# A hybrid decoder step on one core: scaling products moved to GpSimd, gate rows asked for a tile earlier, a raw buffer for the output weights, and half of the sample rows' output products ahead

## The chip, the cores and the metric

The kernel runs on one core of a Trainium2 chip. The metric is the device time of one execution in microseconds (us). The core has five engines that work side by side, each through its own queue in order: TensorE (PE, with its weight loads as PEld), VectorE (DVE), ScalarE (ACT), GpSimd (POOL) and SyncE (SP, which here issues most DMAs). SBUF is the working memory of 128 partitions, PSUM the memory into which PE writes.

## The reference, cut to what matters

One inference step for a prompt of 1024 rows and for 8 sample rows with a cache of 1024 rows each. A row goes through one input projection, then through three groups of heads, and through one output projection.

```python
q_raw, kv_raw, g_raw, z_nsa, u_rw, z_rw, q_mem, z_mem = split_in(rms_norm(hp, ln_g[l]) @ w_in[l])
o_nsa = ...    # 8 heads: compressed blocks, selected blocks, a window of 512, mixed by gates
o_rw, sh_p, st_p = rwkv7_mix(u_rw, ...)                     # 4 heads, a recurrence
o_mem = mem_attend(q_mem, mkv_p, mem_q_norm[l])             # 4 heads against 256 memory rows

def mixer_out(o_nsa, z_nsa, o_rw, z_rw, o_mem, z_mem, w_out):
    cat = jnp.concatenate([o_nsa.reshape(b, t, NSA_W) * jax.nn.silu(z_nsa),
                           o_rw * jax.nn.silu(z_rw),
                           o_mem.reshape(b, t, MEM_W) * jax.nn.silu(z_mem)], axis=-1)
    return cat @ w_out
hp = hp + mixer_out(...)
```

The softmaxes are `p = exp(s - m)` and `p / sum(p)`. The division by the sum is the scaling that this change moves between engines.

## The kernel before

There are three phases. Phase 1 (0 to about 515 us) projects all rows and runs the recurrence. Phase 2 (about 515 to 822) is the attention of the prompt rows: eight tiles of 128 rows, from tile 7 down to tile 0, each with four units (a key head and a pair of query heads). For a unit PE makes scores `p_s`, DVE masks them and takes their maximum (L1321), ACT takes the exponential into `p` (L1322), DVE takes the reciprocal of the sum `fac` (L1344), GpSimd scales `p` by it and the gate (L1347), PE transposes it into `p_pT`, DVE or ACT copies that to `pt` (L1294, L1292), PE multiplies by the values into `p_o`, and DVE multiplies the result into `cat` (L1380), which starts out as the gate rows z. Beside the units run smaller pieces as Python generators, which hand over when PE's modelled clock has moved on by the number that they yield: `q_stack` (queries split into a high and a low part, `qhl`, and transposed into `qs`), `attn_cmp` (the compressed branch: scores `p_sc`, softmax `pcq`), `attn_rwkv` (the recurrence's rows `y_rw`, transposed into `p_yT` and multiplied into `cat`, L1280), `attn_mem` (memory attention: `p_sm`, softmax `pmem`, transposed into `p_pTm`), and the sample rows' own small tasks. `load_z` asks for one tile's `y_rw` and gate rows by two DMAs.

Phase 3 (822 to the end) weaves two generators together. `out_prompt` is the output projection of the prompt rows: first the output columns of half 1 with the weights W1, then half 0 with W0. `wo_half` loads and splits the weights of a half in eight pieces k: a DMA into one of three buffers `wor`, a high part `woh` on ACT (L2191) and a low part `wol` on DVE (L2192). `out_rows` makes 24 matmuls `p_out` of a tile and half and adds the residual `xres`. `sample_nsa` is the attention of the sample rows over their cache pages `pg`, in two fours (a = 0, 1); `pages` issues the DMAs of a sample, `squeeze` compresses a sample's cache (`p_hid`), `nsa_four` does four samples' attention from `p_ss` on. At the end `out_proj_sample` zeroes and fills `c_s`, the sample rows' concatenated outputs `cats` in high and low parts, and makes 32 `p_out` matmuls with W0 and with W1, whose pieces are loaded and split a second time, since W0 took over the space of the first.

PE's instructions are kept in the order in which the generators emit them. On the other engines a scheduler sets the order from the same sequence, and pieces marked with a high priority (`first`) come ahead. The order on every engine thus follows from the yields and from the places of the calls.

Of the kernel before, what the change touches and what calls it, by code (L numbers as in the profile page):

```python
# [114 lines left out]
class Step:  # L115
# [1054 lines left out]
    def prompt_cmp(self):  # L1170
# [43 lines left out]
    def q_stack(self, i):  # L1214
        nc = self.nc
        A, G, PE = nc.scalar, nc.gpsimd, self.te
        first = i == 7
        q = self.kt.tile([128, 12, 64], F32, name="q7") if first else self.we.tile([128, 12, 64], F32, name="q", tag="q", bufs=2)
        nc.sync.dma_start(q[:].rearrange("p h d -> p (h d)"), self.q_d[i * 128:(i + 1) * 128, :])
        qs = self.qs[i] = (self.kt if i % 2 else self.wk).tile([128, 12, 128], F32R, name="qs", tag="qs")  # L1220
        for b in (0, 1, 2):
# [2 lines left out]
            A.activation(hl[:, :, 0], q[:, 4 * b:4 * b + 4], AF.Copy)
            (self.nc.vector if i < 3 else G).tensor_tensor(hl[:, :, 1], q[:, 4 * b:4 * b + 4], hl[:, :, 0].bitcast(F32), op=OP.subtract)
# [4 lines left out]
            yield  # L1230

    def load_z(self, i):
        cat = self.cat[i] = self.slot(i, [128, 8, 128], F32, f"cat{i}")
        y = self.y_rw[i] = self.we.tile([128, 256], F32, name="y_rw", bufs=2)
        self.nc.sync.dma_start(y[:], self.y_d[i * 128:(i + 1) * 128, :])
        self.last_z = self.nc.sync.dma_start(cat[:], self.z_d[:, i * 128:(i + 1) * 128].rearrange("(c p) t -> p c t", p=128))

    def attn_cmp(self, i):
# [30 lines left out]
        V.tensor_tensor(pcq[:], pcq[:], bc(rc[:, :, None], [128, 8, 64]), op=OP.mult)  # L1269
        yield 6.0 if i < 7 else 4.0  # L1270
# [111 lines left out]
    def attn_mem(self, i):  # L1382
# [5 lines left out]
        for c in range(2):  # L1388
# [13 lines left out]
            V.tensor_tensor(pm[:], pm[:], bc(sm[:, :, None], [128, 2, 256]), op=OP.mult)  # L1402
# [73 lines left out]
    def phase2(self):  # L1476
        tc, nc, I, O = self.tc, self.nc, self.I, self.O
        with ExitStack() as ctx:
# [77 lines left out]
            for j, (n, a, b) in enumerate(groups):  # L1556
                i, g, hp = units[n]
                self.unit = n
                if a == 0:
                    left = sum(1 for m, _, _ in groups if m == n)  # L1560
                    if (g, hp) == (0, 0):
# [4 lines left out]
                        if i < 7:  # L1566
                            self.load_z(i)
# [615 lines left out]
    def wo_half(self, pool, n, queue):  # L2183
        nc, I = self.nc, self.I
        out = []
        for k in range(8):
            wl = pool.tile([128, 512], F32R, name=f"wol{k}")
            raw = self.wst.tile([128, 512], F32, name="wor")[:]
            self.last_wor = queue.dma_start(raw, I["w_out"][0, k * 128:(k + 1) * 128, n * 512:(n + 1) * 512])
            wh = pool.tile([128, 512], F32R, name=f"woh{k}")  # L2190
            nc.scalar.activation(wh[:], raw, AF.Copy, scale=0.5)  # L2191
            nc.vector.scalar_tensor_tensor(wl[:], raw, 0.5, wh[:].bitcast(F32), op0=OP.mult, op1=OP.subtract)  # L2192
            out.append((wh, wl))
# [32 lines left out]

    def out_proj_sample(self, Ws):

        nc, I, O = self.nc, self.I, self.O
        c = self.op.tile([128, 8, 40], F32R, name="c_s", tag="chi", bufs=2)  # L2230
        z = self.op.tile([128, 8, 40], F32, name="c_z", tag="clo", bufs=2)
        nc.gpsimd.memset(z[:], 0.0)
        nc.gpsimd.tensor_copy(c[:], z[:])
        nc.scalar.activation(c[:, :, 0:NS], self.cats, AF.Copy)
        nc.vector.tensor_tensor(c[:, :, 32:40], self.cats, c[:, :, 0:NS].bitcast(F32), op=OP.subtract)
        for n, W in enumerate(Ws):
            cs = slice(n * 512, n * 512 + 512)
            o = self.op.tile([128, 512], F32, name="xres", bufs=3)
            nc.sync.dma_start(o[:NS], I["x_sample"][:, 0, cs])
            po = self.pP.tile([128, 512], F32, name="p_out", tag="o")  # L2240
            for k in range(8):
                for j in range(2):
                    self.te.matmul(po[:40], c[:, k, :], W[k][j][:], start=(k == 0 and j == 0), stop=(k == 7 and j == 1))
            nc.vector.tensor_tensor(o[:NS], o[:NS], po[:NS], op=OP.add)
            nc.vector.tensor_tensor(o[:NS], o[:NS], po[32:40], op=OP.add)
            nc.sync.dma_start(O["y_sample"][:, 0, cs], o[:NS])
# [8 lines left out]
    def phase3(self):  # L2255
        tc = self.tc
        with ExitStack() as ctx:
# [4 lines left out]
            self.wst = P("wst", 3)  # L2262
# [108 lines left out]
```

## Time and profile before

| | us |
|---|---|
| median of 3 runs (lowest, highest) | 983.46 (983.21, 985.57) |
| the profiled execution, by its own time | 988.05 |
| span of the profiled execution | 986.3 |
| mean granted TensorE clock | 0.993 |

The span goes from the first to the last instruction. A row of the profile names a line of the kernel, an engine, an operation, and its tiles as out<-in. "xN" counts instructions; behind "<-" stands what released a waiting instruction. The table of windows gives each engine's busy time within a stretch, the granted TensorE clock as a share of full speed, the share of time that the DMA engines were busy, and GB/s. The rows themselves stand in the prediction.

### The profile page before, as it was taken

The page shows a single profiled execution, that of the slowest core. Times are in us where ns is not written, and L with a number is a line of the kernel's source. Part 1 is how long each engine was busy: PE and PEld are TensorE (multiplying, and loading weights), DVE is VectorE, ACT ScalarE, POOL GpSimd, SP SyncE. Part 2 cuts the span into 40 slices and gives each one's busy share as a digit, 9 for nine tenths or more (in the row PEclk, how much of TensorE's full clock was granted, in tenths as well). Part 3 has the DMA queues.
Part 4 walks back from the last instruction along what each step waited for, and adds up shares of the span by engine and source line. Part 5 has one row for each costly group of instructions (what it writes and reads, how often), then busy time and mean ns, then how long its engine had stood idle before and what let it go on. Part 6 is the DMA issues. An engine that isn't in the chain of part 4 may idle for free.

```text
span 986.3 us, 24664 instructions
## 1 busy us (share of the span) xinstructions
PE 934.6 (95%) x9851; PEld 788.9 (80%) x9851; DVE 673.2 (68%) x2056; ACT 442.4 (45%) x989; POOL 153.3 (16%) x222
## 2 busy tenths in 40 slices
PE   7999999999999998999998999989999998999997
PEld 7998888878888887788876878878878885877874
DVE  6769579756683997643448668765879986357465
ACT  6664224233522333223435666646577565224212
POOL 2000000000000000000004332423244542112010
PEclk9999999999999999999999999999999999999999
DMA  8321314212221144147148223321210127984512
GB/s 287 105 68 39 92 32 121 76 46 74 74 90 36 39 139 98 45 132 187 44 120 241 94 74 122 126 77 40 54 36 16 61 76 203 300 280 162 161 66 77
DMA packets 133835, 103.81 MB, mean 105 GB/s; under 512 B 34577, under 2 KB 121112, under 8 KB 133592
## 3 DMA queue, kind: packets, MB, share of 16 engines
q1 hardware_dynamic: 128760, 90.53, 31.5%
q0 software_dynamic: 3200, 10.49, 3.2%
q8 instruction: 78, 1.28, 0.5%
q10 hardware_dynamic: 1760, 1.21, 0.4%
q14 instruction: 37, 0.30, 0.1%
HBM read 83.61 MB, written 22.78 MB: 108 GB/s over the span
## 4 chain that ended last, share of the span: by engine, by line
PE 67%; DVE 15%; ACT 7%; DMA 5%; issue 3%; SPq 2%; POOL 0%; ACTq 0%; DVEq 0%; POOLq 0%
PE p_pr L87 20%; PE p_pr L284 8%; PE p_out L87 5%; PE p_pT L87 5%; PE p_s L87 5%; PE p_o L87 4%; ACT p L1322 3%; PE p_hid L87 2%; DMA x<-in_x_prompt_dram 2%; PE p_iy L87 2%; PE p_z L87 1%; DVE p L1321 1%; PE p_it L87 1%; DVE pt L1294 1%; PE p_sc L87 1%
## 5 line engine op out<-in xcount | busy, mean ns | idle before, releaser
L87 PE MATMUL p_pr<-h,whi 128*128 128x512 f32 (+5 forms) x928 | 231.0, 340 | 0.1
L87 PEld LDWEIGHTS p_pr<-h,whi 128*128 128x128 f32 (+1 forms) x928 | 147.3, 184 | 18.8 <-issue 2.7
L87 PE MATMUL p_pr<-h,wlo 128*128 128x512 f32 (+5 forms) x464 | 152.5, 329 | 0.0
L1347 POOL TENSOR_SCALAR p<-p,fac,gates 128x640 f32<-128x640 f32 (+7 forms) x128 | 109.4, 866 | 162.9 <-DVE fac L1344 104.2
L1322 ACT ACTIVATE p<-p,nm 128x640 f32<-128x640 f32 (+7 forms) x128 | 93.0, 728 | 61.4 <-DVE nm L1321 52.8
L87 PEld LDWEIGHTS p_pr<-h,wlo 128*128 128x128 f32 (+1 forms) x464 | 85.1, 183 | 9.6
L284 PE MATMUL p_pr<-h,whi 128*128 128x256 f32 (+2 forms) x416 | 86.8, 304 | 0.4 <-ACT whi L273 0.3
L87 PE MATMUL p_pT<-ident,p 128*128 128x128 f32 x528 | 72.6, 281 | 8.6 <-DVE cat L1280 2.7
L87 PEld LDWEIGHTS p_pT<-ident,p 128*128 128x128 f32 x528 | 57.4, 141 | 20.6 <-issue 8.7
L1321 DVE CUSTOM_DVE_ANT_0 p<-p_s,bmask 128x512 f32<-128x512 f32 (+7 forms) x96 | 60.3, 663 | 13.5 <-PE p_s L87 6.2
L284 PEld LDWEIGHTS p_pr<-h,whi 128*128 128x128 f32 x416 | 66.1, 188 | 3.6 <-ACT whi L273 0.7
L87 PE MATMUL p_o<-pt,vs 128*64 128x128 f32 x1056 | 67.9, 277 | 0.4 <-DVE shid L1009 0.4
L87 PE MATMUL p_s<-kh,qs 128*128 128x512 f32 (+3 forms) x191 | 66.6, 361 | 1.3 <-DVE nm L1321 1.3
L274 DVE TENSOR_TENSOR wlo<-wraw,whi 128x1024 fp32r<-128x1024 f32 (+1 forms) x34 | 40.7, 1197 | 36.1 <-ACT whi L273 36.1
L87 PEld LDWEIGHTS p_o<-pt,vs 128*64 128x64 f32 x1056 | 57.0, 137 | 7.5 <-issue 4.4
L284 PE MATMUL p_pr<-h,wlo 128*128 128x256 f32 (+2 forms) x208 | 62.6, 303 | 0.0
L998 POOL MEMSET w2d<- 128x128 f32 x1 | 0.2, 206 | 399.2 <-PE p_yy L87 399.2
L87 PE MATMUL p_s<-kl,qs 128*128 128x512 f32 (+3 forms) x192 | 61.3, 339 | 0.0
L273 ACT ACTIVATE whi<-wraw 128x1024 fp32r<-128x1024 f32 (+1 forms) x35 | 36.3, 1038 | 50.1 <-PE p_pr L87 36.7
L1294 DVE COPY pt<-p_pT 128x512 f32<-128x512 f32 (+1 forms) x72 | 47.9, 669 | 10.7 <-PE p_pT L87 9.5
L87 PE MATMUL p_out<-woh,chi 128*128 128x512 f32 x128 | 53.7, 419 | 1.3 <-ACT woh L2191 1.3
L87 PE MATMUL p_out<-wol,chi 128*128 128x512 f32 x128 | 51.9, 406 | 1.2 <-DVE wol L2192 0.9
(534 smaller groups left out, 1936.0 us busy)
## 6 DMA issues: line engine op xcount, KB each, us to landing
wraw<-in_w_in_dram SPq DMA_DIRECT2D x34, 512.0 KB
pg<-in_c_pool_dram SPq DMA_DIRECT2D x40, 256.0 KB
pg<-in_c_pool_dram SPq DMA_DIRECT2D x48, 128.0 KB
x<-in_x_prompt_dram SPq DMA_DIRECT2D x8, 512.0 KB
z_d<-zt SPq DMA_DIRECT2D x16, 256.0 KB
cat<-z_d SPq DMA_DIRECT2D x8, 512.0 KB
wor<-in_w_out_dram SPq DMA_DIRECT2D x16, 256.0 KB
xres<-in_x_prompt_dram POOLq DMA_DIRECT2D x16, 256.0 KB, 3.7
```

Source lines behind the costliest of these rows:

```text
L87: self.last = getattr(self.engine, op)(*a, **k)
L273: nc.scalar.activation(hi[:, :, :n], raw[:, :, :n], AF.Copy)
L274: (low or nc.vector).tensor_tensor(lo[:, :, :n], raw[:, :, :n], hi[:, :, :n].bitcast(F32), op=OP.subtract)
L284: self.last_mm = self.pe.matmul(ps[:m, :b - a], w[:, k, :m], h[k][:, a:b], start=(k == 0 and i == 0), stop=(k == 7 and i == 2))
L998: nc.gpsimd.memset(w2d[:], 0.0)
L1294: nc.vector.tensor_copy(pt[:, :n], ps[:, :n])
L1321: V.tensor_tensor_reduce(halves(x), halves(ps), m, -1.0, 3.0e38, op0=OP.add, op1=OP.min, accum_out=nm[:, h, b:b + 1])
L1322: A.activation(x, x, AF.Exp, scale=-1.0, bias=nm[:, h, b:b + 1], accum_out=sm[:, h, b:b + 1])
L1347: nc.gpsimd.tensor_scalar(x, x, f[:, h, b:b + 1], gate[:, hd + h, 1 + b:2 + b], op0=OP.mult, op1=OP.mult)
```

## The change

1. Scaling moves from DVE to GpSimd: `pmem`'s (one product of 128x512 becomes two of 128x256, by the reciprocal and a constant `one`), `pcq`'s for the tiles 6 to 0, and the subtraction of `qhl` for the tiles 2 to 0 (it was on GpSimd already for the others).
2. `load_z` is called for tile i-1 when tile i begins, with three `y_rw` buffers for two, and `attn_cmp` yields 7 for 6.
3. In phase 3 W1's eight pieces are loaded into one raw buffer `wraw`, each in a place of its own. Later two samples' value pages use it, so that `big` has 5 slots for 7, and samples 4 and 5 load their pages by two DMAs each.
4. `sample_cats` fills the second half of `c_s` (k 4 to 7, the recurrence's and the memory's columns) after the first four samples. W1's pieces 4 to 7 are loaded again and split during the second four, and pieces 0 to 3 later. `out_proj_sample` makes the products of k 4 to 7 for both halves, then fills k 0 to 3 and makes the rest.

```diff
@@ q_stack
-            (self.nc.vector if i < 3 else G).tensor_tensor(hl[:, :, 1], q[:, 4 * b:4 * b + 4], hl[:, :, 0].bitcast(F32), op=OP.subtract)
+            G.tensor_tensor(hl[:, :, 1], q[:, 4 * b:4 * b + 4], hl[:, :, 0].bitcast(F32), op=OP.subtract)
@@ load_z
-        y = self.y_rw[i] = self.we.tile([128, 256], F32, name="y_rw", bufs=2)
+        y = self.y_rw[i] = self.we.tile([128, 256], F32, name="y_rw", bufs=3)
@@ attn_cmp
-        V.tensor_tensor(pcq[:], pcq[:], bc(rc[:, :, None], [128, 8, 64]), op=OP.mult)
-        yield 6.0 if i < 7 else 4.0
+        (G if i < 7 else V).tensor_tensor(pcq[:], pcq[:], bc(rc[:, :, None], [128, 8, 64]), op=OP.mult)
+        yield 7.0 if i < 7 else 4.0
@@ attn_mem
-            V.tensor_tensor(pm[:], pm[:], bc(sm[:, :, None], [128, 2, 256]), op=OP.mult)
+            for h in range(2):
+                G.tensor_scalar(pm[:, h, :], pm[:, h, :], sm[:, h:h + 1], self.one[:], op0=OP.mult, op1=OP.mult)
@@ phase2
-                        if i < 7:
-                            self.load_z(i)
+                        if i == 7:
+                            self.load_z(6)
+                        if i > 0 and i < 7:
+                            self.load_z(i - 1)
@@ sample_nsa
+            raw = ctx.enter_context(tc.tile_pool(name="wraw", bufs=1, reuse_waits="tile", side="right")).tile(
+                [128, 2, 2048], F32, name="wraw")
+            self.W1 = self.wo_half(self.wo_tiles(self.wop), 1, nc.sync, range(8),
+                                   lambda k: raw[:, k // 4, k % 4 * 512:k % 4 * 512 + 512])
...
-                big = xp.tile([128, 7, 2048], F32, name="pg")
+                big = xp.tile([128, 5, 2048], F32, name="pg")
...
-                        load(4)
-                        load(5)
+                        for s in (4, 5):
+                            self.pages(s, big[:, 5 - s], raw[:, s - 4])
+                            X[s], KV[s] = big[:, 5 - s], kvs(raw[:, s - 4])
...
+                        again = [self.k1p.tile([128, 2048], F32R, name="wob", tag=f"k{j}") for j in (0, 2)]
+                        parts = iter([x[:, k * 512:k * 512 + 512] for x in again for k in range(4)])
+                        W1 = self.wo_half(lambda name: next(parts), 1, nc.sync, range(4, 8),
+                                          lambda k: big[:, 0, k * 512:k * 512 + 512])
...
                     if a == 0:
+                        self.sample_cats()
                         yield None
-            W1 = self.wo_half(ctx.enter_context(P("wop2")), 1, nc.sync)
+            W1 |= self.wo_half(self.wo_tiles(ctx.enter_context(P("wop2"))), 1, nc.sync, range(4))
@@ wo_half
+            raw = self.wst.tile([128, 512], F32, name="wor")[:] if raws is None else raws(k - ks[0])
@@ out_proj_sample
+        for a in (4, 0):
+            if a == 0:
+                self.split_sample(0, 4)
+            for n, W in enumerate(Ws):
+                po = pos[n]
+                for k in range(a, a + 4):
+                    for j in range(2):
+                        self.te.matmul(po[:40], self.c_s[:, k, :], W[k][j], start=(k == 4 and j == 0), stop=(k == 3 and j == 1))
```

In the new order the lines of the kernel have moved by a few: what was L1280 is L1282, L1347 is L1349, L1402 is L1405, L2189 is L2204.

**DVE, tile 4 of the prompt attention**, before: the end of the window branch of a sample task (`rs_s`, `w_p`), the end of the compressed branch (`c_s`, `c_r`, `pcq`), then the recurrence's rows into `cat`.

```order
L1699 TENSOR_REDUCE rs_m<-p_wS 128x1
L1259 TENSOR_TENSOR pcq<-p_sc,c_m 128x512
L1344 RECIPROCAL fac<-sm 128x2
L1702 RECIPROCAL rs_s<-rs_s 128x1
L1704 TENSOR_TENSOR rs_s<-rs_s,gr 128x1
L1705 TENSOR_SCALAR w_p<-w_p,rs_s 128x512
L1263 TENSOR_REDUCE c_s<-pcq 128x8
L1266 TENSOR_SCALAR c_r<-c_s 128x8
L1267 RECIPROCAL c_r<-c_r 128x8
L1268 TENSOR_TENSOR c_r<-c_r,gates 128x2x4
L1269 TENSOR_TENSOR pcq<-pcq,c_r 128x512
L1280 TENSOR_TENSOR cat_8885<-cat_8885,p_yT 128x256
```

The same place on DVE in the changed kernel, from the reduction of the window branch on:

```order
L1704 TENSOR_REDUCE rs_m<-p_wS 128x1
L1282 TENSOR_TENSOR cat_8136<-cat_8136,p_yT 128x256
L1707 RECIPROCAL rs_s<-rs_s 128x1
L1709 TENSOR_TENSOR rs_s<-rs_s,gr 128x1
L1710 TENSOR_SCALAR w_p<-w_p,rs_s 128x512
L1323 ISA p,nm<-p_s,bmask 128x640
L1323 ISA nm 128x1
L1259 TENSOR_REDUCE c_m<-p_sc 128x8
```

The product into `cat` now follows the reduction directly, and the compressed branch begins only after it.

**GpSimd, tile 2 of the prompt attention** (its p products are 128x384), in the changed kernel. Before, there stood sixteen p products in a row here and nothing else.

```order
L1349 TENSOR_SCALAR p<-p,fac,gates 128x384 x2
L1405 TENSOR_SCALAR pmem<-pmem,sm_m,one 128x256 x2
L1349 TENSOR_SCALAR p<-p,fac,gates 128x384 x2
L1405 TENSOR_SCALAR pmem<-pmem,sm_m,one 128x256 x2
L1227 TENSOR_TENSOR qhl<-q,qhl 128x4x64
L1349 TENSOR_SCALAR p<-p,fac,gates 128x384 x4
L1227 TENSOR_TENSOR qhl<-q,qhl 128x4x64
```

The products of pmem and the subtractions of qhl now stand between the p products, each of which has to wait for those ahead of it.

**SyncE, the start of phase 3**, in the changed kernel: the last weights of the compression, W1's eight pieces, the sample rows' new values, and the first page of a sample (a load of its number, then the DMA).

```order
L1238 DMA cat_11007<-z_d 128x8x128
L960 DMA w1a<-in_cmp_w_dram 128x8x64 x4
L2204 DMA wraw<-in_w_out_dram 128x512 x8
L1889 DMA v_new<-out_dram 32x2x128 x4
L1852 TENSOR_LOAD pt
L1856 ISA
L1856 DMA pg<-in_c_pool_dram 128x2x256
```

Before, the four v_new DMAs stood ahead of the weights, and the eight weight loads, into `wor`, each had their own wait.

More of the change, by code (lines that the diff above doesn't have):

```diff
@@ L1133, in key_pools @@
         self.bmask = self.kt.tile([128, 1152], BF, name="bmask")
+        self.one = self.kt.tile([128, 1], F32, name="one")
         self.qs, self.pcT, self.y_rw, self.turn, self.cat = {}, {}, {}, 0, {}
@@ L1175, in prompt_cmp @@
         G.memset(self.bmask[:], 0.0)
+        G.memset(self.one[:], 1.0)
         V.tensor_copy(self.bmask[:, 0:128], am[:, 128:256])
@@ L1890, in sample_nsa @@
             with P("snsx") as xp:
-                big = xp.tile([128, 7, 2048], F32, name="pg")
-                at = {1: (0, 2), 2: (1, 3), 3: (0, 4), 4: (1, 5), 5: (0, 6)}
+                big = xp.tile([128, 5, 2048], F32, name="pg")
+                at = {1: (0, 2), 2: (1, 3), 3: (0, 4)}
                 kvs = lambda x: x.rearrange("p (n c) -> p n c", n=8)
@@ L2180, in sample_rwkv, with wo_half, wo_tiles @@
         yield
[L2183 to L2193, printed above, removed]
-        return out
+    def wo_half(self, tiles, n, queue, ks=range(8), raws=None):
+        nc = self.nc
+        out = {}
+        for k in ks:
+            wl, wh = tiles(f"wol{k}"), tiles(f"woh{k}")
+            raw = self.wst.tile([128, 512], F32, name="wor")[:] if raws is None else raws(k - ks[0])
+            self.last_wor = queue.dma_start(raw, self.I["w_out"][0, k * 128:(k + 1) * 128, n * 512:(n + 1) * 512])
+            nc.scalar.activation(wh, raw, AF.Copy, scale=0.5)
+            nc.vector.scalar_tensor_tensor(wl, raw, 0.5, wh.bitcast(F32), op0=OP.mult, op1=OP.subtract)
+            out[k] = wh, wl
+        return out
+    def wo_tiles(self, pool):
+        return lambda name: pool.tile([128, 512], F32R, name=name)[:]
     def out_rows(self, W, hi, lo, rows, x, dst):
@@ L2201, in out_rows @@
             for j, (c, w) in enumerate(((hi, wh), (hi, wl), (lo, wh))):
-                self.te.matmul(po[:rows], c[:, k, :rows], w[:], start=(k == 0 and j == 0), stop=(k == 7 and j == 2))
+                self.te.matmul(po[:rows], c[:, k, :rows], w, start=(k == 0 and j == 0), stop=(k == 7 and j == 2))
             if k < 7:
@@ L2225, in out_proj_prompt, with sample_cats @@
             yield
-    def out_proj_sample(self, Ws):
[L2229 to L2246, printed above, removed]
+    def sample_cats(self):
+        x = self.k1p.tile([128, 2048], F32R, name="c_s", tag="k1")
+        self.c_s = x[:, 0:320].rearrange("p (c s) -> p c s", s=40)
+        self.nc.gpsimd.tensor_scalar(self.c_s, self.cd[:].rearrange("p (c s) -> p c s", s=40), 0.0, 0.0, op0=OP.mult, op1=OP.add)
+        self.split_sample(4, 8)
@@ new lines, in split_sample @@
+    def split_sample(self, a, b):
+        nc, c = self.nc, self.c_s
+        nc.scalar.activation(c[:, a:b, 0:NS], self.cats[:, a:b], AF.Copy)
+        nc.vector.tensor_tensor(c[:, a:b, 32:40], self.cats[:, a:b], c[:, a:b, 0:NS].bitcast(F32), op=OP.subtract)
+    def out_proj_sample(self, Ws):
+        nc, O = self.nc, self.O
+        pos = [self.pP.tile([128, 512], F32, name="p_out", tag="o") for _ in Ws]
+        os = [self.op.tile([128, 512], F32, name="xres", bufs=3) for _ in Ws]
+        for n, o in enumerate(os):
+            nc.sync.dma_start(o[:NS], self.I["x_sample"][:, 0, n * 512:n * 512 + 512])
+        for a in (4, 0):
[6 more added lines that the diff above has]
+                        self.te.matmul(po[:40], self.c_s[:, k, :], W[k][j], start=(k == 4 and j == 0), stop=(k == 3 and j == 1))
+                if a == 0:
+                    o = os[n][:NS]
+                    nc.vector.tensor_tensor(o, o, po[:NS], op=OP.add)
+                    nc.vector.tensor_tensor(o, o, po[32:40], op=OP.add)
+                    nc.sync.dma_start(O["y_sample"][:, 0, n * 512:n * 512 + 512], o)
@@ L2248, in out_prompt @@
     def out_prompt(self):
         yield from self.out_proj_prompt(1, self.W1)
-        self.W0 = self.wo_half(self.wop, 0, self.nc.gpsimd)
+        self.W0 = self.wo_half(self.wo_tiles(self.wop), 0, self.nc.gpsimd)
         self.half = 1
@@ L2261, in phase3 @@
             self.tk = self.wk
-            self.wst = P("wst", 3)
+            self.wst = P("wst", 3, side="right")
             self.wop = P("wop", 1)
@@ L2268, in phase3 @@
             self.pP = P("pP3", 2, space=PSUM)
-            self.W1, self.half = self.wo_half(self.wop, 1, tc.nc.sync), 0
+            self.half = 0
             self.te = InOrder(tc, tc.nc.tensor, None)
```

## The prediction

> **What bounds the kernel now.** I read the busy shares and the chain first, to see which engine a change has to help.
>
> ```profile
> PE 934.6 (95%) x9851; PEld 788.9 (80%) x9851; DVE 673.2 (68%) x2056; ACT 442.4 (45%) x989; POOL 153.3 (16%) x222
> PE 67%; DVE 15%; ACT 7%; DMA 5%; issue 3%; SPq 2%; POOL 0%; ACTq 0%; DVEq 0%; POOLq 0%
> ```
>
> TensorE (PE) is busy 95% of the span, and no edit takes a matmul away. A gain can only come out of the time in which PE waits or runs at a lower clock. GpSimd (POOL) looks free at 16%, but that is an average. So the next view is the windows, for the stages that the change touches: the end of the prompt attention (760 to 820), the start of phase 3 (820 to 860) and its second four samples (920 to 940).
>
> ```profile
> core 0: us, PE busy (x) PEld busy (x) DVE busy (x) ACT busy (x) POOL busy (x), PEclk, DMA share, GB/s
> 760.00:780.00 20.00, 18.63 (x199) 16.66 (x199) 19.84 (x52) 13.39 (x38) 14.02 (x13) 1.00 0.10 35
> 780.00:800.00 20.00, 18.11 (x186) 15.77 (x182) 19.03 (x70) 13.65 (x44) 10.03 (x16) 1.00 0.38 107
> 800.00:820.00 20.00, 18.14 (x203) 15.38 (x203) 16.63 (x80) 11.91 (x46) 7.47 (x16) 1.00 0.37 86
> 820.00:840.00 20.00, 17.28 (x112) 11.73 (x107) 12.59 (x25) 9.99 (x17) 3.99 (x7) 0.93 0.73 215
> 840.00:860.00 20.00, 20.00 (x115) 17.50 (x114) 5.48 (x11) 3.75 (x7) 2.17 (x4) 0.99 0.97 311
> 920.00:940.00 20.00, 19.31 (x111) 14.71 (x111) 6.91 (x16) 4.16 (x8) 2.17 (x4) 1.00 0.55 168
> ```
>
> From 760 to 820 VectorE (DVE) is busy 55.5 of 60 us and POOL already 31.5 of 60, while PE idles 5.1 us. Which waits carry PE's idle time after 500 us says the view of waits:
>
> ```profile
> PE p_pT L87 <- DVE cat L1280: 2.7, 1, 2.7
> PE p_out L87 <- DVE c_s L2235: 2.5, 1, 2.5
> PE p_pT L87 <- DVE pcq L1269: 2.4, 1, 2.4
> PE p_out L87 <- ACT woh L2191: 1.3, 3, 0.8
> PE p_ss L87 <- DMA pg<-in_c_pool_dram: 0.7, 1, 0.7
> ```
>
> The first is in tile 4 of the prompt attention, the second at the very end, the fourth at the start of phase 3; the change reaches all three. The third belongs to tile 7, whose pcq product stays on DVE, and remains. The fifth is one that the change may lengthen.
>
> **First output weights.** W1 comes through three buffers `wor`, so its fourth load waits for the first split.
>
> ```profile
> 816.79 2.45 SPq L1880 DMA_DIRECT2D v_new<-out_dram  x4
> 819.34 13.50 SPq L2189 DMA_DIRECT2D wor<-in_w_out_dram  x8
> 833.42 37.01 SPq L1851 DMA_DIRECT2D pg<-in_c_pool_dram  x32
> ```
>
> ```profile
> 830.03 0.63 ACT L2191 ACTIVATE woh<-wor 128x512 fp32r<-128x512 f32 x1 [1.06 <-DMA wor<-in_w_out_dram]
> 830.69 0.69 DVE L2192 SCALAR_TENSOR_TENSOR wol<-wor,woh 128x512 fp32r<-128x512 f32 x1 [1.04 <-ACT woh L2191]
> ```
>
> ```profile
> 827.10:837.90 10.80, 8.57 (x25) 4.31 (x26) 0.00 (x0) 0.97 0.69 201
> 837.90:840.50 2.60, 2.60 (x8) 2.01 (x7) 0.69 (x1) 0.50 0.96 269
> 840.50:846.00 5.50, 5.50 (x26) 4.55 (x25) 0.69 (x1) 0.99 1.02 345
> ```
>
> The first two fences are SyncE's queue and the two halves of a split, each with what it waited for; the third cuts out the p_out matmuls alone. The eight loads take 13.50 us to issue, ACT waits for each (1.06 us in the row), and 25 matmuls need 10.80 us where 26 need 5.50 a little later. So 10.80 less 25 x 0.21, or 5.5 us, is lost, and then 2.60 us go at a granted clock of 0.50, which loses 1.3 more. Now the eight loads go into `wraw` without waiting for each other and stand ahead of v_new on SyncE's queue, so they issue from about 816.8. 2.1 MB at the 311 GB/s of the row of 840 to 860 are 6.7 us: they land by about 826, or up to 5 us later if GpSimd's three W0 and three xres loads (1.6 MB) share the DMA engines all along. DVE's halves then set the pace: 8 x 0.69 = 5.5 us beside its other work, about as fast as PE uses them. I take back 0.3 for that: **-6.5 us**, between 0 (the loads are late all the same) and -6.8. v_new and the pages move along: the pages start near 823 rather than 833.42, and the 128 KB pages of samples 4 and 5, which now take two issues each, are needed only after 900, so they cost nothing unless SyncE stays busy past that time.
>
> **The gap in tile 4.** DVE, in order, does the end of the compressed branch before it comes to the product that ends PE's longest wait:
>
> ```profile
> 651.66 0.69 DVE L1269 TENSOR_TENSOR pcq<-pcq,c_r 128x512 f32<-128x512 f32 x1
> 652.27 0.41 DVE L1280 TENSOR_TENSOR cat<-cat,p_yT 128x256 f32<-128x256 f32 x1
> 652.74 1.05 PE L87 MATMUL p_pT<-ident,p 128*128 128x128 f32 x4 [2.69 <-DVE cat L1280]
> 650.00:655.00 5.00, 2.31 (x11) 2.26 (x11) 3.94 (x10) 0.60 (x1) 1.08 (x1) 0.79 0.00 0
> 655.00:660.00 5.00, 4.97 (x56) 4.33 (x55) 3.04 (x9) 2.72 (x6) 1.74 (x2) 0.87 0.01 3
> ```
>
> In the changed order cat<-p_yT comes ahead of that chain, since its cat was asked for a tile earlier and pcq's product is on GpSimd. Of the 2.69 us I count **-2.5**. The half clock behind it, 5 x 0.21 + 5 x 0.13, is another **-1.7**. What is late next there is the window branch's w_p (L1705), which in the new order follows cat<-p_yT.
>
> The clock row bears on a rule: the half clock in 650 to 660 comes after an idle time of 2.69 us. The Trainium skill, "TensorE: Matmul & The Clock Gate", "What's actually happening", gives an idle window of about 3.4 us as what lowers the clock; by that page's rule this gap would not lower it, and the clock terms (1.7 and 1.3) would not hang on these gaps. The trace disagrees in this place: the gap is shorter and the clock fell.
>
> **Scaling on GpSimd.** What moves, and what the nearest operations take:
>
> ```profile
> L1402 DVE TENSOR_TENSOR pmem<-pmem,sm_m 128x512 f32<-128x512 f32 x16 | 12.2, 760 | 0.2
> L1269 DVE TENSOR_TENSOR pcq<-pcq,c_r 128x512 f32<-128x512 f32 x8 | 6.1, 767 | 0.1
> L1225 DVE TENSOR_TENSOR qhl<-q,qhl 128x256 fp32r<-128x256 f32 x9 | 3.7, 415 | 5.3 <-ACT qhl L1224 5.3
> L1347 POOL TENSOR_SCALAR p<-p,fac,gates 128x256 f32<-128x256 f32 x16 | 10.4, 667 | 10.7 <-DVE fac L1344 7.8 <-PE p_q L87 2.9
> L1225 POOL TENSOR_TENSOR qhl<-q,qhl 128x256 fp32r<-128x256 f32 x12 | 8.8, 731 | 31.8 <-PE p_s L87 19.2 <-ACT qhl L1224 12.5
> ```
>
> DVE loses 12.2 + 7 x 0.767 + 3.7 = 21.3 us. In tiles 2 to 0, the stretch from 760 to 820, that is 3 x (2 x 0.76 + 0.767 + 3 x 0.415) = 10.6 of its 55.5. PE idles 5.1 us there, the most that this can give back; the least is nothing. I take **-1.5**, since only part of that idle time ends with DVE.
>
> GpSimd gets 32 pmem halves (nearest row: 0.667 us each), 9 subtractions (0.731) and 7 pcq products of 128x512, which it doesn't do before: between one 128x256 product (0.731) and more than two of them (1.46 and up, to 2.4 if blocked); I take 1.2. For tiles 2 to 0 that is 12 x 0.667 + 9 x 0.731 + 3 x 1.2 = 18.2 us on top of 31.5, so 49.7 of 60. It fits, but p's own scaling, for which PE's transposes wait, now queues behind these: waits of **+1.5** in all, between 0 and what the rival below gives.
>
> ```profile
> L1347 POOL TENSOR_SCALAR p<-p,fac,gates x13: 559/686/1707, 760.9 to 779.6; 128x384 f32<-128x384 f32 x12, 128x256 f32<-128x256 f32 x1
> ```
>
> This row of line 1347 alone, for 760 to 780, has the minimum, median and maximum of one operation: 0.56 to 1.71 us, nearly all of one shape. GpSimd is slowed up to 2.5 times where DVE is never idle. The Trainium skill, "SBUF — State Buffer", "Who interferes with whom", says that a DVE instruction with two SBUF inputs and a GpSimd one that reads SBUF exclude each other for the whole instruction, which speaks against this part of the change. The trace agrees in size; by that rule, if every added operation met such an instruction, the sum would be the rival's, below.
>
> At the last tile the order changes too: two pmem halves stand before the last two p products and two after, 2 x 0.667 where DVE took 0.76: **+0.7**, as nothing else covers it. The memset of `one`, and c_s's zeroing after the first four samples, lie on GpSimd where it idles: nothing.
>
> **Second four samples and end.** Four W1 loads are inserted on SyncE among the last value pages, for which p_ss waits already.
>
> ```profile
> 645.10 0.43 SPq L1236 DMA_DIRECT2D cat<-z_d  x1
> 913.44 21.07 SPq L1855 DMA_DIRECT2D pg<-in_c_pool_dram  x24
> ```
>
> A load costs SyncE 0.43 us in the nearest row for a plain one, and 0.88 as a page: 1.7 to 3.5 us, or nothing if the pages are early now. I take **+1.7**. Their splits (4 x 0.63 on ACT, 4 x 0.69 on DVE) lie in 920 to 940, where DVE is busy 6.91 of 20; if that cover were gone they would cost 2.8.
>
> ```profile
> 973.91 0.67 DVE L2207 TENSOR_TENSOR xres<-xres,p_out 128x512 f32<-128x512 f32 x1
> 974.78 0.43 PE L87 MATMUL p_out<-woh,c_s 128*40 128x512 f32 x1 [2.47 <-DVE c_s L2235]
> 980.13 4.00 SPq L2246 DMA_DIRECT2D out_dram<-xres  x2
> ```
>
> PE waits 2.47 us for c_s. Now 16 matmuls of k 4 to 7 (3.5 us at 0.22) stand in that wait; the second half's PSUM buffer comes free only when the xres add ends (974.58), some 0.5 us of waiting. So **-2.0**, between 0 and -2.5.
>
> **Sum:** -6.5 - 2.5 - 1.7 - 1.5 + 1.5 + 0.7 + 1.7 - 2.0 = -10.3 us. The profiled execution took 988.05 (span 986.3), so it would be 977.8; the median of the runs is 4.6 lower than it, and the same -10.3 gives 983.46 - 10.3 = **973.2**.
>
> **Rivals.** 0.3%, 2.95 us, is about what a measurement can tell from no change: faster ends at 980.5, slower begins at 986.4.
>
> 1. *Phase 2 gives its part back.* The new order makes other gaps, with half clocks behind them, for the one it closes. For it: DVE's 55.5 of 60 leave every order tight. Against: pmem and pcq are used late. Then only -6.5 + 1.7 - 2.0 = -6.8 is left, 976.7, to 979 with one gap of 2.5 more. Chance 0.22.
> 2. *W1 is still late:* wraw's space comes free only after the last p_s, and eight loads compete with W0, xres and the pages (DMA share 0.97 in 840 to 860). Half of the 6.5 would go: 976.5, or 979.7 if all of it does. It is also the case in which the change doesn't do what it says. Chance 0.12.
> 3. *GpSimd becomes the bound in tiles 2 to 0*, the slower side. The 18.2 added us fit if they stretch less than (60 - 31.5)/18.2 = 1.57 times; at the 2.5 times of the row (1707 to 686) they are 45.5, 77 of 60, so that phase lasts 17 us longer. With the other terms (-6.5 - 2.5 - 1.7 + 0.7 + 1.7 - 2.0 = -10.3): +6.7, 990. Against it: most p rows have the median, not the maximum; at 2.1 times it is even. Chance 0.14, of which 0.10 slower.
>
> The forecast has 0.52. **Faster** gets 0.52 + 0.20 + 0.06, **same** 0.02 + 0.06 + 0.04, **slower** 0.10. The range goes from 966 (DVE's relief whole, the p_ss wait and the GpSimd waits nothing: -3.6 - 1.7 - 1.5) to 982, which takes in both phase-3-only cases and a mild form of rival 3.
>
> **What would show it.** The p_out group near 820 to 835 has no waits for woh, and pages start near 823; if ACT waits for `wraw`, rival 2. No wait of p_pT for cat<-p_yT and a clock of 1.00 in tile 4; new waits over 2 us between 515 and 820 mean rival 1, and p_pT waiting for POOL's p with POOL over 55 of 60 means rival 3. p_ss waits for a page near 2.4 us. The last p_out matmuls follow p_oT directly. I am wrong as a whole if GpSimd's 128x512 product takes far over 1.2 us, or if PE's half clocks come at new places.

## The result, and the profile after

| | before | changed |
|---|---|---|
| median of 5 runs each on one chip, us | 983.46 | 978.97 |
| lowest to highest | 983.21 to 986.12 | 976.72 to 983.03 |
| ratio changed to before, 95% interval | | 0.9942 (0.9918 to 0.9966) |
| the profiled execution, its own time | 988.05 | 983.03 |
| its span | 986.3 | 981.3 |
| its mean granted TensorE clock | 0.993 | 0.984 |

The kernel is faster by 4.5 us, or 0.58%; the forecast was 10.3 us. The profiled execution of the changed kernel is the longest of its five, with the lowest clock (the others had 0.989 to 0.995). First the busy shares and the chain of the changed kernel:

```profile
PE 939.0 (96%) x9851; PEld 796.3 (81%) x9851; DVE 656.6 (67%) x2025; ACT 443.1 (45%) x990; POOL 178.9 (18%) x270
PE 72%; DVE 15%; ACT 6%; DMA 3%; issue 2%; SPq 1%; POOL 0%; DVEq 0%; ACTq 0%; POOLq 0%
```

GpSimd took 25.6 us more, DVE 16.6 less, and PE's share of the chain rose. PE's longest waits after 500 us:

```profile
PE p_ss L87 <- DMA pg<-in_c_pool_dram: 2.6, 1, 2.6
PE p_PT L87 <- DVE s_sel L1710: 2.5, 2, 1.9
PE p_pT L87 <- DVE pcq L1271: 2.3, 1, 2.3
...
PE p_sm L87 <- DVE pt L1296: 1.3, 1, 1.3
...
PE p_pT L87 <- POOL p L1349: 1.0, 1, 1.0
```

The waits for cat (2.7) and c_s (2.5) are gone, and that for woh has fallen from 1.3 to 0.5. The wait of p_ss has become the longest, 2.6 for 0.7 us, and p_sm waits for a pt copy (near 600 us) where no such wait stood. SyncE's queue and the p_out matmuls at the start of phase 3:

```profile
812.50 6.20 SPq L2204 DMA_DIRECT2D wraw<-in_w_out_dram  x8
818.81 3.44 SPq L1889 DMA_DIRECT2D v_new<-out_dram  x4
822.90 25.99 SPq L1856 DMA_DIRECT2D pg<-in_c_pool_dram  x20
826.10:831.60 5.50, 5.38 (x24) 4.48 (x25) 0.00 (x0) 1.00 1.04 330
```

The eight loads issue in 6.20 us, the pages follow at 822.90, and 24 p_out matmuls take 5.50 us at full clock. The windows of the granted clock, and the end, first the p_oT matmul of the profile before, then the changed kernel:

```profile
520.50:530.70 10.20, 10.20 (x33) 8.40 (x33) 7.78 (x17) 5.46 (x11) 3.81 (x4) 0.50 0.86 241
930.10:933.50 3.40, 0.85 (x7) 0.00 (x1) 0.63 (x2) 0.00 (x0) 0.02 (x1) 1.00 0.52 189
933.50:936.90 3.40, 3.37 (x9) 1.74 (x10) 0.00 (x0) 0.00 (x0) 0.51 (x1) 0.50 0.23 77
936.90:940.30 3.40, 3.40 (x17) 2.81 (x17) 2.75 (x13) 0.42 (x1) 0.00 (x0) 1.00 0.00 0
```

```profile
972.03 0.27 PE L87 MATMUL p_oT<-ident,oS 128*128 128x128 f32 x1
```

```profile
968.98 0.27 PE L87 MATMUL p_oT<-ident,oS 128*128 128x128 f32 x1
969.00 0.47 PE L87 MATMUL p_out<-woh,c_s 128*40 128x512 f32 x1
971.58 2.05 PE L87 MATMUL p_out<-wob,c_s 128*40 128x512 f32 x8 [0.49 <-DVE xres L2224]
976.95 2.15 SPq L2274 DMA_DIRECT2D out_dram<-xres  x2
```

Just behind the wait of p_ss the clock goes to 0.50 for one window of 3.4 us. 10 us at half clock also stand from 520.5 to 530.7, where the profile before had none; PE is busy all through them. At the end the matmuls follow p_oT at once, with the wait of 0.49 for the xres add.

### The profile page after: what moved, and what is told of

Its sections match the earlier page's. It is cut to its first block, busy times and chain, and to the rows that moved or that the text cites. A ratio compares the mean times of both kernels' runs of the same rounds, so it can differ in the third digit from the quotient of the medians.

```text
span 981.3 us, 24739 instructions
## 1 busy us (share of the span) xinstructions
PE 939.0 (96%) x9851; PEld 796.3 (81%) x9851; DVE 656.6 (67%) x2025; ACT 443.1 (45%) x990; POOL 178.9 (18%) x270
## 4 chain that ended last, share of the span: by engine, by line
PE 72%; DVE 15%; ACT 6%; DMA 3%; issue 2%; SPq 1%; POOL 0%; DVEq 0%; ACTq 0%; POOLq 0%
PE p_pr L87 20%; PE p_pr L284 7%; PE p_out L87 6%; PE p_s L87 6%; PE p_pT L87 4%; PE p_o L87 4%; PE p_hid L87 3%; ACT p L1324 2%; DVE p L1323 2%; PE p_iy L87 2%; PE p_sc L87 2%; PE p_z L87 1%; PE p_it L87 1%; PE p_mo L1077 1%; PE p_w L203 1%
## 5 line engine op out<-in xcount | busy, mean ns | idle before, releaser
L1349 POOL TENSOR_SCALAR p<-p,fac,gates 128x640 f32<-128x640 f32 (+7 forms) x128 | 103.7, 821 | 108.5 <-DVE fac L1346 62.1
L273 ACT ACTIVATE whi<-wraw 128x1024 fp32r<-128x1024 f32 (+1 forms) x35 | 36.3, 1038 | 50.4 <-PE p_pr L87 36.7
```

The source lines that it names most:

```text
L273: nc.scalar.activation(hi[:, :, :n], raw[:, :, :n], AF.Copy)
L1349: nc.gpsimd.tensor_scalar(x, x, f[:, h, b:b + 1], gate[:, hd + h, 1 + b:2 + b], op0=OP.mult, op1=OP.mult)
```

## The experiments

Each group of kernels (e1 to e4, e5 to e8, e9 to e12) ran on a chip of its own, and each ratio is to the kernel before in the same group. The last columns come from the mean granted clock c that each run lists: T x (1 - c) is the time that PE lost if it was the bound all along, and twice that by 3.41 us, the length of one window in the traces, the number of windows at half clock. Within one kernel, over all 206 runs, a run with one microsecond more of T x (1 - c) is 0.64 us longer (correlation 0.79). "At full clock" is the mean time less 0.64 x T x (1 - c); errors are standard errors of the mean. The 0.64 is a correlation, and a late transfer could lengthen a run and lower its clock at once; the one direct test is e12 against e11. The count also takes in half clock behind PE's last matmul, where it costs nothing (in e4's profile 1.0 of 7.8 us). The 81 runs before are those of the three groups, with medians of 986.1, 986.3 and 985.5.

| kernel | runs | median us | ratio to before, 95% interval | mean us | half-clock windows | mean at full clock |
|---|---|---|---|---|---|---|
| before | 81 | 986.0 | | 986.2 ± 0.3 | 3.8 ± 0.2 | 982.0 ± 0.2 |
| changed (first 5 runs and e4; ratio of e4) | 17 | 979.0 | 0.9936 (0.9909, 0.9963) | 980.1 ± 0.8 | 5.9 ± 0.6 | 973.7 ± 0.4 |
| e1 phase 2 alone | 12 | 984.1 | 0.9969 (0.9946, 0.9991) | 983.7 ± 0.7 | 4.2 ± 0.5 | 979.1 ± 0.4 |
| e2 phase 3 alone | 12 | 982.2 | 0.9955 (0.9931, 0.9978) | 982.5 ± 0.8 | 5.2 ± 0.5 | 976.8 ± 0.4 |
| e3 W1 behind pages | 12 | 980.0 | 0.9931 (0.9903, 0.9959) | 980.6 ± 1.0 | 5.7 ± 0.8 | 974.5 ± 0.5 |
| e5 scaling alone | 6 | 982.2 | 0.9952 (0.9933, 0.9971) | 982.2 ± 0.6 | 4.3 ± 0.6 | 977.4 ± 0.4 |
| e6 z ahead alone | 12 | 984.5 | 0.9984 (0.9967, 1.0001) | 984.9 ± 0.6 | 4.3 ± 0.6 | 980.2 ± 0.4 |
| e7 filled wait | 6 | 979.7 | 0.9919 (0.9892, 0.9945) | 978.9 ± 1.2 | 3.9 ± 0.7 | 974.6 ± 0.7 |
| e8 W1 by GpSimd's queue | 6 | 979.7 | 0.9935 (0.9910, 0.9959) | 980.1 ± 1.1 | 5.4 ± 0.8 | 974.2 ± 0.6 |
| e9 changed, no z ahead | 6 | 978.7 | 0.9924 (0.9895, 0.9953) | 978.6 ± 0.6 | 4.9 ± 0.4 | 973.2 ± 0.5 |
| e10 W1 behind, GpSimd splits | 12 | 986.7 | 1.0009 (0.9987, 1.0030) | 986.1 ± 0.7 | 6.9 ± 0.3 | 978.6 ± 0.5 |
| e11 e9 with e10 | 12 | 984.7 | 0.9992 (0.9970, 1.0014) | 985.5 ± 0.7 | 7.2 ± 0.5 | 977.7 ± 0.4 |
| e12 e11, tile 7 filled | 12 | 983.5 | 0.9975 (0.9956, 0.9994) | 983.6 ± 0.6 | 5.5 ± 0.3 | 977.5 ± 0.4 |

**The two halves of the change (e1, e2).** e1 has only the edits 1 and 2 of the change, e2 only 3 and 4.

> Only the edits of phase 2 (scaling on GpSimd, z rows a tile ahead); phase 3 as before. Theory 1 (the prediction's sum): -1.8 us from waits and -1.7 where a half clock went, so about 980 to 982 beside 983.46. Theory 2 (the profile of the changed kernel: phase 2 lasted 304.9 us for 307.4 although it held 8.5 us of half clock loss for 3.4): the waits alone save 7 to 8 us, so 976 to 977 in runs with a mean clock as high as before, and more where the clock is lower. Theory 3 (phase 2 gave its part back): 983 or more.

> Only the edits of phase 3; phase 2 as before. Theory 1: -6.5 for W1, +1.7 at p_ss, -2.0 at the end, so about 976.7. Theory 2 (the profile of the changed kernel, counted from p_new to the end): 159.7 for 163.8 us, so -4 us, 979.4, because p_ss waits 2.6 us and not 0.7, with a half clock behind it. The first pages after W1 must start within 5 us of the end of phase 2 under both.

At full clock the halves are worth 3.0 and 5.2 us, and the whole 8.3, with errors of about 0.4 each: they add up. Theory 1 has the size of e2 at full clock (-6.8 without the 1.3 of the half clock is -5.5). Theory 2 for e1 is too large, and so was its reading of one profile: a span of 304.9 with half clocks subtracted isn't a price. Measured as they run, with their half clocks, e1 gives 2.5 and e2 3.7 us on the means.

**The same kernel again (e4).**

> The changed kernel once more, unaltered, with a profile of its own. If half clocks fall at random places from run to run, this profile has them at other places than 520 to 531, 537, 817, 896 and 933 us, and runs with a lower mean clock are longer by about half of a half-clock window (1.7 us) each. If they hang on the gaps that the change made, they are at the same places.

Its profiled execution has a span of 974.8 us at a clock of 0.992. The half clock at p_ss is there again, one window longer, that near 817 and 896 isn't:

```profile
922.00:925.10 3.10, 0.98 (x10) 0.07 (x3) 0.86 (x2) 0.37 (x1) 0.00 (x0) 1.00 0.69 246
925.10:931.90 6.80, 5.90 (x16) 3.78 (x17) 1.87 (x8) 0.42 (x1) 0.54 (x1) 0.50 0.11 41
```

So both expectations hold in part: most half clocks stand behind places where PE does little, and which of these places gets one changes from execution to execution. Not all do. The rows below are e4's, and then those of e7, a kernel described further down:

```profile
512.20:515.60 3.40, 1.75 (x9) 1.10 (x7) 3.40 (x25) 1.29 (x6) 0.00 (x0) 1.00 0.38 121
519.00:522.40 3.40, 2.57 (x15) 1.59 (x14) 3.32 (x7) 1.84 (x4) 0.11 (x1) 0.99 1.01 265
522.40:525.80 3.40, 3.40 (x7) 2.30 (x8) 2.42 (x6) 3.40 (x8) 2.70 (x3) 0.51 1.06 325
```

```profile
689.90:693.30 3.40, 3.40 (x30) 3.11 (x28) 1.76 (x6) 0.26 (x2) 0.89 (x2) 1.00 0.19 52
693.30:696.80 3.50, 3.50 (x27) 3.19 (x28) 2.06 (x7) 1.74 (x5) 0.00 (x0) 0.51 0.96 246
```

In e4 the clock stayed at 1.00 after 3.4 us in which PE was busy 1.75, and fell after 3.4 us in which it was busy 2.57; in e7 it fell where the profile shows no idle time of PE at all. What else lowers it these runs don't show. Runs of the changed kernel go from 976.6 to 986.9 us.

**Scaling and z ahead apart (e5, e6, e9).** e5 takes the GpSimd edits alone, e6 the z edits alone, and e9 undoes the z edits in the changed kernel:

```diff
-        y = self.y_rw[i] = self.we.tile([128, 256], F32, name="y_rw", bufs=3)
+        y = self.y_rw[i] = self.we.tile([128, 256], F32, name="y_rw", bufs=2)
-                        if i == 7:
-                            self.load_z(6)
-                        if i > 0 and i < 7:
-                            self.load_z(i - 1)
+                        if i < 7:
+                            self.load_z(i)
-        yield 7.0 if i < 7 else 4.0
+        yield 6.0 if i < 7 else 4.0
```

> Only the scaling products on GpSimd (pmem, pcq, qhl); z rows, yields and phase 3 as before. Theory 1 (the prediction's terms: -1.5 for DVE, +1.5 for waits behind GpSimd, +0.7 at the last tile): +0.7 us against before. Theory 2: DVE's relief is worth more, -2 us or better, since p_q and p_pTm no longer wait for DVE. The gap of 2.7 us in tile 4 goes already here if it hung on the pcq chain on DVE, and stays if it hung on where cat<-p_yT stands.

> Only the z rows a tile ahead and the yield of 7; scaling and phase 3 as before. Theory 1: the gap in tile 4 goes, -2.5 us, and with it its half clock. Theory 2: the pcq chain still stands ahead on DVE in another tile, and the gap comes back elsewhere: within 1 us of before.

> The changed kernel with z rows asked for when their tile begins, two y_rw buffers and the yield of 6, as before; scaling and phase 3 as changed. Theory 1 (the prediction: z ahead closes the gap in tile 4, worth 2.5 us): 2 to 3 us slower than the changed kernel. Theory 2 (from e1, e5 and e6: z ahead closes that gap and opens one of 1.7 to 2.5 us at p_sm near 597, so it is worth nothing): within 1 us of the changed kernel, with a gap near 650 and none near 597.

PE's longest waits between 590 and 660 us, the first row of e6, the second of e9:

```profile
PE p_sm L87 <- DVE pt L1294: 1.5, 1, 1.5
```

```profile
PE p_pT L87 <- DVE cat L1282: 2.0, 1, 2.0
```

z ahead closes the wait for cat and opens one at p_sm. Alone it gives 1.9 us at full clock, which as it runs can't be told from nothing (0.9967 to 1.0001). Taken back from the changed kernel (e9) it leaves the time where it was: 973.2 ± 0.5 for 973.7 ± 0.4 at full clock. In e5, too, the wait for cat is 2.0 us (2.7 before), so it hangs on where cat<-p_yT stands and not on the pcq product alone. Scaling alone is worth 4.6 us at full clock and 0.9952 as it runs, where the forecast had a small loss. The two together (e1) gave 1.6 us less than scaling alone, on another chip and with errors of 0.4 each; why they don't add up there wasn't settled. That GpSimd can bear the work shows in the windows, first of the kernel before and then of e5, and in the rows of the p products and the moved ones, first before (line 1347) and then e5:

```profile
740.00:820.00 80.00, 74.59 (x790) 65.29 (x790) 73.55 (x254) 52.69 (x165) 38.63 (x53) 1.00 0.23 62
```

```profile
740.00:820.00 80.00, 75.44 (x826) 66.07 (x824) 68.27 (x243) 54.17 (x167) 47.57 (x72) 1.00 0.26 70
760.00:820.00 60.00, 55.57 (x608) 48.23 (x607) 50.35 (x193) 38.47 (x124) 34.99 (x56) 1.00 0.33 89
```

```profile
L1347 POOL TENSOR_SCALAR p<-p,fac,gates 128x384 f32<-128x384 f32 x16 | 16.6, 1052 | 13.8 <-DVE fac L1344 9.5 <-DVE sm_m L1401 4.3
```

```profile
L1405 POOL TENSOR_SCALAR pmem<-pmem,sm_m,one 128x256 f32<-128x256 f32 x32 | 17.5, 559 | 17.2 <-DVE sm_m L1403 15.4 <-DVE rq_a L126 1.8
L1349 POOL TENSOR_SCALAR p<-p,fac,gates 128x384 f32<-128x384 f32 x16 | 14.2, 903 | 10.8 <-DVE fac L1346 6.4 <-DVE sm_m L1403 4.5
L1349 POOL TENSOR_SCALAR p<-p,fac,gates 128x256 f32<-128x256 f32 x16 | 9.1, 585 | 1.8 <-DVE rq_t L135 1.1 <-DVE fac L1346 0.6
```

From 760 to 820 DVE went from 55.5 to 50.4 of 60 us, GpSimd from 31.5 to 35.0. Part of tile 2's work lies ahead of 760; from 740 on, with all of it, GpSimd went from 38.6 to 47.6 of 80. A pmem half takes 0.559 us, and the p products themselves became faster: 0.903 us at 128x384 (1.052 before) and 0.585 at 128x256 (0.667). Little of the gain lies in the tiles 2 to 0, where the prediction looked for it: from the first p product of tile 3 to that of tile 0 e5's profile takes 79.6 us for 80.8 before. From tile 5 to tile 3 it takes 95.5 for 99.5; 1.7 of that is a half clock that stood there before (652.9 to 656.3).

**The wait of p_ss: is it the cause of half clocks? (e7)** PE gets idle matmuls in the wait, and the order of the p_ss matmuls is such that the last page comes last:

```diff
+                            for n in range(11 * a):
+                                PE.matmul(pS[1][:40], self.c_s[:, 4 + n % 4, :], self.W0[4 + n % 4][0], start=True, stop=True)
```

> The changed kernel with 11 idle matmuls (2.5 us, their results are overwritten) put on PE where p_ss waits for the last page in the second four. If the wait causes half clocks behind it, they vanish there (the granted clock is 1.00 behind p_ss in the profile, lost time in the runs lower by one to two windows' 1.7 us) and the kernel is 1 to 3 us faster than the changed one. If half clocks come at random, the time is the same or longer by what the matmuls overrun the wait (0 to 1 us).

The windows of e7 at the same place, in the same 3.4 us steps:

```profile
925.90:929.30 3.40, 3.40 (x22) 1.34 (x19) 0.85 (x2) 0.58 (x1) 0.00 (x0) 1.00 0.68 233
929.30:932.70 3.40, 3.40 (x19) 2.05 (x16) 0.89 (x3) 0.42 (x1) 0.54 (x1) 1.00 0.24 77
932.70:936.10 3.40, 3.40 (x17) 2.79 (x16) 3.02 (x16) 1.01 (x1) 0.00 (x0) 1.00 0.00 0
```

The half clock at p_ss is gone, and the runs have 3.9 ± 0.7 half-clock windows for 5.9 ± 0.6. That is about two standard errors, and most of the changed kernel's runs are from another chip. The mean is 1.3 us lower than the changed kernel's, which lies within the errors (1.2 and 0.8); the time at full clock is the same within them (974.6 ± 0.7 for 973.7 ± 0.4).

**What makes p_ss wait (e3, e8, e10, e11).** e3 emits the second load of W1's pieces 4 to 7 after the first piece of nsa_four, e8 sends it through GpSimd's queue, and e10 is e3 with the low parts made on GpSimd; e11 is e10 and e9 together.

```diff
-                        again = ...
-                        W1 = self.wo_half(lambda name: next(parts), 1, nc.sync, range(4, 8), ...)
...
-                    yield from self.nsa_four(a, hid, pS, VS, vn, dp)
+                    four = self.nsa_four(a, hid, pS, VS, vn, dp)
+                    yield next(four)
+                    if a == 1:
+                        again = ...
+                        W1 = self.wo_half(lambda name: next(parts), 1, nc.sync, range(4, 8), ...)
+                    yield from four
```

```diff
+            if pool:
+                nc.gpsimd.tensor_scalar(raw, raw, 0.5, 1.0, op0=OP.mult, op1=OP.mult)
+                nc.scalar.activation(wh, raw, AF.Copy)
+                nc.gpsimd.tensor_tensor(wl, raw, wh.bitcast(F32), op=OP.subtract)
```

> The changed kernel, but W1's pieces 4 to 7 are loaded a second time behind the last value pages on SyncE's queue instead of between them. If the four loads alone make p_ss wait, its wait falls from 2.57 us to 0.7 or less and the time by 2 to 3.5 us against the changed kernel (to about 976). If the pages are late for another reason (the issue of 128 KB pages, the half clock), the wait stays above 2 us and the time within 1 us of the changed kernel.

> The changed kernel, but W1's pieces 4 to 7 are loaded the second time through GpSimd's queue instead of SyncE's; their splits stay ahead of s_ck on DVE. If the four loads between the pages make p_ss wait, its wait falls to 1 us or less without the new wait of p_ckT that e3 had, and the time is 2 to 4 us below the changed kernel. If it is the pages' own issue (24 of 0.88 us), the wait stays above 2 us.

> As e3 (W1's pieces 4 to 7 loaded behind the last value pages), but their low parts are made on GpSimd, so that no split stands between s_ck and nr_o on DVE. If e3 lost its gain by those splits on DVE, p_ss waits 0.7 us and p_ckT under 1 us, and the time is 2 to 4 us below the changed kernel. If p_ckT still waits over 2 us, ACT's or the DMAs' part of the splits holds the chain.

> e9 and e10 together: scaling on GpSimd, phase 3 as changed with W1's second load behind the pages and split on GpSimd, no z ahead. If both theories 2 hold, 976 to 978 where the kernel before has 986, with under 4.5 half-clock windows on the mean.

PE's longest waits from 905 us to 935 (e8) or 950 (e3, e10), in the order e3, e8, e10:

```profile
PE p_ckT L87 <- DVE nr_o L376: 2.5, 1, 2.5
PE p_ss L87 <- DMA pg<-in_c_pool_dram: 0.7, 1, 0.7
```

```profile
PE p_hid L87 <- DMA pg<-in_c_pool_dram: 2.4, 1, 2.4
```

```profile
PE p_ckT L87 <- DVE nr_o L376: 9.3, 1, 9.3
```

The four loads between the pages do make p_ss wait: behind the pages they bring its wait back to 0.7 us (e3), and on another queue to nothing (e8). With them between the pages it is 2.6 to 3.0 us in four profiles (changed, e2, e4, e9). Where phase 3 is as before it still varies: 0.7 before, none in e6, 1.2 in e5, 1.6 in e1. But no time is won. In e3 the four splits then stand in DVE's chain from s_ck to nr_o, and p_ckT waits 2.5 us. In e8 another page is late and p_hid waits 2.4. e10 was to clear e3's chain and made it far worse, and e11, for which 976 to 978 us and under 4.5 windows were expected, has 984.7 and 7.2. The rows of e10 on DVE, ACT and GpSimd:

```profile
933.17 0.54 POOL L2232 DMA_DIRECT2D xres<-in_x_prompt_dram  x1 [6.42 <-DMA out_dram<-xres]
933.73 1.21 POOL L2209 TENSOR_SCALAR pg<-pg 128x512 f32<-128x512 f32 x2
934.39 0.63 ACT L2210 ACTIVATE wob<-pg 128x512 fp32r<-128x512 f32 x1 [8.53 <-POOL pg L2209]
934.93 0.40 ACT L352 ACTIVATE nr_sq<-s_ck 128x256 f32<-128x256 f32 x1
936.96 1.27 POOL L2211 TENSOR_TENSOR wob<-pg,wob 128x512 fp32r<-128x512 f32 x1
937.05 1.20 DVE L128 TENSOR_SCALAR rq_a<-rq_a 128x4 f32<-128x4 f32 x1
938.78 2.49 POOL L2211 TENSOR_TENSOR wob<-pg,wob 128x512 fp32r<-128x512 f32 x2
940.10 1.19 DVE L135 TENSOR_TENSOR rq_t<-rq_r 128x4 f32<-128x4 f32 x1
941.33 0.16 DVE L136 TENSOR_TENSOR rq_t<-rq_t,rq_a 128x4 f32<-128x4 f32 x1
```

GpSimd's first split waits behind an xres load, which waits 6.42 us for a buffer; ACT's copy waits for that split; and nr_sq, for which the whole chain waits, stands behind this copy on ACT. Then DVE's small instructions take 1.2 us instead of 0.16 each while GpSimd's products of two tiles run.

**Filling another wait (e12).** e11 with ten idle matmuls ahead of tile 7's p_pT transposes.

```diff
+            for j in range(fill):
+                self.te.matmul(ps[:].rearrange("p a b -> p (a b)"), self.qs[7][:, 0, :], self.kh[0][:, 0, 0:512], start=True, stop=True)
```

> e11 with 10 idle matmuls (2.3 us, results overwritten) on PE in the wait for pcq of tile 7 near 530, which has a half clock behind it in every profile so far. If the wait causes it, the clock is 1.00 from 532 to 540 in this profile and the time 1 to 2 us below e11. If PE is not the bound there (DVE's queue is), the clock rises and the time stays.

The same stretch of time in e11 and in e12, and a second one in e12:

```profile
532.80:536.10 3.30, 2.99 (x12) 2.72 (x13) 2.84 (x10) 0.60 (x1) 1.24 (x1) 0.50 0.93 270
```

```profile
532.80:536.10 3.30, 3.30 (x24) 2.85 (x23) 3.13 (x9) 0.93 (x4) 2.20 (x2) 1.00 0.84 274
522.90:529.70 6.80, 6.46 (x20) 5.06 (x21) 5.28 (x15) 5.26 (x11) 4.44 (x5) 0.50 0.96 289
```

The half clock there is gone. This profile has two other windows at half clock, from 522.9 to 529.7, where e11's has none, so only the runs can tell the price: they have 5.5 ± 0.3 for 7.2 ± 0.5 windows, or 2.8 us less of T x (1 - c), and the mean is 2.0 us lower, with the same time at full clock. Idle matmuls in a wait are thus worth what the half clock behind it costs.

## Why the prediction was right and wrong, point by point

The direction and the range were right; 10.3 us was more than twice the 4.5 measured. On the means of all runs the gain is 6.1: the five runs before had a median of 983.5, where the 81 later ones have 986.0. The measured 979 is also the number that rival 1 gave for one new gap, but not by its mechanism, for phase 2 kept its gain (e1). At full clock the change is worth 8.3 us (982.0 to 973.7), where the prediction's terms without its two half-clock terms (1.7 and 1.3) come to 7.3. That these lie so near is in part luck: within phase 2 a term that was too large (z ahead) and one that was too small (scaling) make up for each other. **The step that failed is the clock.** It took two of the four half-clock windows of the profile away with the gaps ahead of them and added none. These two are indeed gone from both profiles of the changed kernel, but others came, and the prediction's own sign of being wrong, half clocks at new places, is met. The runs have 3.8 windows before and 5.9 after, so that T x (1 - c) grew from 6.5 to 10.0 us. At 0.64 each that is about 2.3 us given back, where 3.0 were counted as won.

- *W1, -6.5.* Right. 24 p_out matmuls take 5.50 us where 25 took 10.80, and the pages start at 822.90 (forecast 823). Rival 2 fell. That 823 came out is luck: the loads began at 812.50 and not at 816.8, and took 6.20 us to issue where the forecast left them under 4.
- *The gap in tile 4, -2.5 and -1.7.* The wait for cat went, but a wait at p_sm came for it, and e9 shows that z ahead adds nothing to the rest. This is rival 1's mechanism, in one place and not in all. It was listed, and not summed.
- *DVE's relief and GpSimd's cost, together +0.7.* Mis-sized: e5 measured -4.6 at full clock. GpSimd's price was taken too high (0.667 us a pmem half, measured 0.559; 1.2 a pcq product, measured 1.04 in the changed kernel, below), and the p products became faster, probably because the products that left DVE were among those that slowed them. So rival 3, which needed them to stretch 1.57 times, had no ground: GpSimd is busy 35.0 of 60 us in e5 (and 47.6 of 80 from 740 on), not 49.7 of 60.
- *p_ss, +1.7.* The wait grew by 1.9 us in one profile (2.6 for 0.7) and by 2.3 in the other of the changed kernel, more than was taken but within the bounds, and for the reason named (e3, e8), though up to 0.9 of it comes and goes without the loads (e1). What wasn't counted is the half clock behind it, which e2, without any edit in phase 2, has as well (from 932 to 939; 5.2 windows in its runs).
- *The end, -2.0.* Right: from p_oT to the end of the span 12.3 us (981.3 - 968.98), before 14.3 (986.3 - 972.03).

The changed kernel's own rows for the moved products:

```profile
L1405 POOL TENSOR_SCALAR pmem<-pmem,sm_m,one 128x256 f32<-128x256 f32 x32 | 17.4, 554 | 13.5 <-DVE sm_m L1403 12.2 <-DVE rq_g L127 1.3
L1271 POOL TENSOR_TENSOR pcq<-pcq,c_r 128x512 f32<-128x512 f32 x7 | 7.3, 1043 | 12.0 <-DVE c_r L1270 8.2 <-DVE nm L1323 1.9 <-DVE rw_b L2098 1.8
```

Where the other added windows come from is open in part: filling p_ss took two away in e7, about what the change had added, but the profiles of the changed kernel, e3, e5, e7 and e8, among others, also have one to three between 518 and 531 us, and those of before, e1, e2, e6 and e11 have none there. e1 and e5 have nearly the same work there, so it may be no more than where the 3.4 us steps fall in an execution. Of the nine windows in the first profile of the changed kernel two even stand from 18.7 to 25.6 us, in phase 1, long ahead of phase 2, in which the changed order begins. e7 and e9 are the fastest versions (0.9919 and 0.9924), both below the kernel before; neither can be told from the changed kernel. The two together weren't run.

## What to carry to other kernels

A profile is one execution: before a half clock in it is subtracted, count it over the clocks of many runs, and expect it to move: most follow 3.4 us in which PE does little, wherever an edit or the execution puts them, but some here did not. A DMA put between others on a queue costs whoever waits for the last of them, and to move it away pays only if its consumers don't then stand in a chain that PE waits for. Where a pair of engines hinders each other, moving work from the one to the other can speed up both (e5).

## What the runs showed of the hardware

- PE's clock fell to 0.50 for one or more windows of 3.4 us behind windows in which PE was busy 0.85 of 3.40 us (changed kernel, 930.1 to 933.5) or 0.98 of 3.10 (e4), without ever having been idle for a whole one: the longest waits there were 2.6 and 3.0 us. It did not fall where the same stretch was filled with idle matmuls (e7, e12). The Trainium skill, "TensorE: Matmul & The Clock Gate", "What's actually happening", asks for one idle window of about 3.4 us; the trace has the same step of 3.4 us, but a window that is three quarters idle was enough. Emptiness isn't all of it: the clock also fell behind 3.4 us in which PE was busy 2.57 (e4, 522.4) and 3.40 (e7, 693.3), and stayed at 1.00 behind 1.75 (e4, 515.6).
- DVE instructions of 128x4 took 1.20 and 1.19 us beside GpSimd products of two tiles (1.27 us, and two in 2.49), and 0.16 when these were over (e10). The Trainium skill, "SBUF — State Buffer", "Who interferes with whom", has the shared port as a lock for the whole instruction; the trace agrees: the first of the two ended at 938.25, with the product beside it (938.23).
- Two runs of one kernel on one chip can differ by 10 us (976.6 and 986.9 for e4) with no edit at all.
